# A fifth buffer for gathered rows, a later mask, norm scaling on another engine, and a new order of all instructions

## The chip, the cores and the metric

The kernel runs on one core of a Trainium2 chip. The metric is the device time of one execution in microseconds (us). Of three runs of the kernel before, the median is 3445.88 us (3432.36 to 3452.61).

The engines' names: PE is TensorE (matmuls; PEld are its weight loads), DVE is VectorE, ACT is ScalarE, POOL is GpSimd, SP is SyncE, which issues most transfers. Each engine works through a queue of its own, in order, and waits on semaphores for the others.

## The reference

One layer of a hybrid network over 1024 latent tokens with a prefix of 256 context tokens, width 1024, all in float32:

```python
h  = modulate(x, norm1_g, mod[:, 0], mod[:, 1])         # rms_norm(x, g) * (1 + scale) + shift
hc = modulate(ctx, norm1_g, mod_c[:, 0], mod_c[:, 1])
rq, rk, rv, rg, dq, dk, dv = split(h @ w_in)            # the same of hc for the context
ret  = bidirectional retention of 4 heads, chunks of 128 (scores * decay mask), rms_norm, * silu(rg)
diff = attention of 4 head pairs: (softmax(q1 k1) - lam * softmax(q2 k2)) @ v, rms_norm
x  = x + mod[:, 2] * (concat([ret, diff]) @ w_out)
h2 = modulate(x, norm2_g, mod[:, 3], mod[:, 4])
x  = x + mod[:, 5] * peer_ffn(h2)

def block_fn(hb):                                        # peer_ffn, per block of 128 tokens
    q = (hb @ w_query).reshape(t, 8, 2, 128)
    s = einsum('thpc,hpnc->thpn', q, sub_keys)
    v1, i1 = top_k(s[:, :, 0], 16); v2, i2 = top_k(s[:, :, 1], 16)
    best, pos = top_k(v1[..., :, None] + v2[..., None, :], 16)      # of 256 sums
    experts = (i1 * 128 + i2) at pos; gate = softmax(best)
    act = gelu(einsum('thkd,td->thk', expert_u[experts], hb))
    return einsum('thk,thkd->td', gate * act, expert_v[experts])
```

There are 16384 experts, each a row of 1024 numbers in `peer_u` and one in `peer_v`. Each token uses 8 heads x 16 = 128 of them.

## The kernel before, in words

Tokens go in 8 blocks of 128 (the context in two more). The program is written as Python generators, but not run in that order. A class `Plan` records every operation as a node, and a list scheduler fixes the order of each engine's queue ahead of time from estimated costs; it tries several passes and keeps the best by its own estimate. All instructions are then issued from one line, so that nearly every row of the profile says L590, and tiles, not lines, tell operations apart. What steers the scheduler are tables of numbers: QSPAN, ASPAN, GSPAN, LSPAN, HSPAN (where in a stage the generators of another stage are woven in), HOLD (a stretch of planned time in which POOL issues no gathers), PACES (due times of the gathers' steps), `bufs` (how many buffers each tag has in SBUF).

The stages:

- Start: the conditioning vectors `cc` go through silu into `sc`, and `mm<-wst,sc` matmuls make the modulation from chunks of `w_mod`. `norm_rows` loads a block of tokens, sums its squares on ACT in two halves, adds the halves on DVE, takes the power -1/2 on POOL, and multiplies the block by that scale. It is called 18 times: five times into a tile of tag `k`, five into `gat`, eight into `wst`. Transposes on PE (`mm<-ident,k` and the like) follow.
- Input projections (each float32 product as three products of split numbers), rotary embedding, retention for the 4 retention heads with the decay mask, attention for groups of blocks [0], [4, 5], [6, 7], [3], [1, 2]. `late_queries` computes some of the queries later (`mm<-wst,rv`, 256 columns).
- `route`, `top16`, `select`: for a block, the scores against the sub-keys and the three top-16 searches. `select` is a run of short DVE instructions on tiles `sel`, ending in `egb` (indices and gates). POOL adds the candidate sums for it.
- Blocks 0, 1 and 2 fetch their experts' rows: `halves` and `gather` issue 768 indirect transfers of 128 rows x 1024 numbers on POOL. A row of `peer_u` is used by one DVE instruction (`gat<-gat,h2t`, a product and its sum), a row of `peer_v` by another (`acc<-gat,act,acc`). Nearly all land in a tile of tag `gat`, which has four buffers and is free again after that DVE instruction; 20 land in buffers lent by tag `h`.
- Blocks 3 to 7 use all experts densely: `gates` writes their gates as a table `Wd`, `dense_act` (128 chunks) splits the chunk's weights on ACT (`CAST h<-wst`) and DVE (`TENSOR_TENSOR h<-wst,h`, the low part) and multiplies (`mm<-k,h`, `mm<-v,h`), `dense_val` multiplies by `peer_v`. This dense phase ends the program; the gathers' DVE work runs beside it.

Of the kernel before, what the change touches and what calls it, by code (L numbers as in the profile page):

```python
# [11 lines left out]
AF = mybir.ActivationFunctionType  # L12
OP = mybir.AluOpType
# [17 lines left out]
PASSES, SHARES = 7, (0.3, 0.5)  # L31
HOLD = [1000, 1550]
EXTRA = [[], [], []]
# [18 lines left out]
LATE = [2, 4, 7]  # L52
QSPAN = [[-0.2, 0.475], [0.1, 1], [-0.1, 1.309], [-0.35, 1.05], [0.15, 0.9]]
ASPAN = [[0.05, 1.424], [0.05, 1.05], [0.15, 1], [0, 1.104]]
GSPAN = [[0.3, 1], [-0.15, 0.754], [0.15, 1.248], [-0.1, 1.2], [-0.3, 0.02]]
DSPAN = [0.02, 0.0, 0.05]
LSPAN = [[0.479, 1.05], [0.565, 1.218], [0.436, 1.3], [0.05, 0.85]]
G2SPAN = [0.182, 0.991]
VL, CL, EC, XE = 'D', 'D', 'D', 'PPPPPPPP'
POFF, PACES = 40, [[0, 3.6], [200, 2.25], [300, 1.17], [700, 1.18], [1100, 1.9]]  # L60
DENSE = [3, 4, 5, 6, 7]
# [6 lines left out]
W0 = [0.552, 1.085]  # L68
HSPAN = [[-0.25, 1.0], [0.05, 0.796], [0.2, 1.588]]
XT = ['gat'] * 5  # L70
# [91 lines left out]
class Plan:  # L162
# [169 lines left out]
    def schedule(self):  # L332
# [77 lines left out]
        while left_n:  # L410
# [22 lines left out]
            for e in engs:  # L433
# [159 lines left out]
def row_bcast(ap, n, offset=0):  # L593
    return bass.AP(tensor=ap.tensor, offset=ap.offset + offset, ap=[[0, 128], [1, n]])


def layer(tc, I, out, dbg=None):
# [3 lines left out]
    with sp as S, pp as P, dp as DR:  # L601
        bufs = {"mm": 8, "h": 8, "k": 5, "rv": 4, "b": 4, "v": 5, "sel": 3, "wst": 4, "gat": 4, "fin": 2,  "u1": 3, "u2": 2, "u3": 2,
                "o": 1, "vi": 2, "egb": 3, "pt": 2, "m4": 4, "s1": 2, "act": 2,  "gsum": 2, "rs": 2, "ssum": 2, "ff": 3}

# [6 lines left out]
        nc = Plan(tc, pools, bufs, {"mm": RESERVE})  # L611
# [4 lines left out]
        def sb(shape, tag, dt=F32):  # L616
            return nc.tile(shape, dt, tag)
# [38 lines left out]

        cc = sb([128, KD, 2], "cc")
        nc.sync.dma_start(cc[:, :, 0], I["c"].rearrange("o (p k) -> (o p) k", k=KD))
# [16 lines left out]
        def norm_rows(kb, tag):  # L675
            lat = kb >= NCB
            src = I["x"][0, (kb - NCB) * 128:(kb - NCB + 1) * 128, :] if lat else I["ctx"][0, kb * 128:(kb + 1) * 128, :]
            xt = sb([128, D], tag)
            nc.sync.dma_start(xt, src)
            junk = ps([128, 512])  # L680
            ms = sb([128, 3], "m4")
            for i in range(2):
                nc.scalar.activation(junk, xt[:, i * 512:(i + 1) * 512], AF.Square, scale=1.0 / 32.0,
                                     accum_out=ms[:, i:i + 1])
            nc.vector.tensor_tensor(out=ms[:, 0:1], in0=ms[:, 0:1], in1=ms[:, 1:2], op=OP.add)
            rstd(ms[:, 2:3], ms[:, 0:1])
            nc.vector.tensor_scalar(xt, xt, ms[:, 2:3], None, op0=OP.mult)
            return xt
# [3 lines left out]
        nc.tensor.transpose(rt, rows, ident[0:24, 0:24])  # L692
        rcol = sb([128, 24], "rcol")
        nc.vector.tensor_copy(rcol, rt)
# [57 lines left out]
        nc.sync.dma_start(sinr, I["k_sin"])  # L752
        dist = sb([128, 2, 128], "vi")
        nc.sync.dma_start(dist, I["k_dist"])
        lg = sb([128, 2, H], "lg")
# [4 lines left out]
        nc.sync.dma_start(lamp.rearrange("p a h -> p (a h)"), row_bcast(I["diff_lambda"], 256))  # L760
        retg = sb([128, 512], "pt")
        nc.sync.dma_start(retg, row_bcast(I["ret_norm_g"], 512))
        difg = sb([128, 512], "difg")
# [3 lines left out]

        t8 = sb([128, 6, 8], "t8")
        lx = lg.rearrange("p a h -> p (a h)")
# [22 lines left out]
        nc.scalar.activation(gC, lg, AF.Exp, scale=128.0)  # L792
        mask = sb([128, H, 128], "pt")
        for h in range(H):
            nc.vector.tensor_scalar(mask[:, h, :], dist[:, 0, :], lg[:, 0, h:h + 1], None, op0=OP.mult)
            nc.vector.scalar_tensor_tensor(mask[:, h, :], dist[:, 1, :], lg[:, 1, h:h + 1], mask[:, h, :],
                                           op0=OP.mult, op1=OP.add)
        nc.scalar.activation(mask, mask, AF.Exp)
        nc.vector.tensor_scalar(mask, mask, SC, None, op0=OP.mult)

# [93 lines left out]
        rv = [rvs[i // 2][:, i % 2, :] for i in range(NKB)]  # L894
# [464 lines left out]
        u2 = I["peer_u"][0]  # L1359
# [57 lines left out]
        def gates(b):  # L1417


            pt, key = pairs[b]  # L1420

            for g in range(128 // TG):
                stage = [sb([128, 32, TG], "gat" if g % 2 else "rv") for _ in range(4)]
                for q in range(TG // 4):
# [207 lines left out]
```

## Time and profile before

| | |
|---|---|
| median of three runs | 3445.88 us (3432.36 to 3452.61) |
| profiled execution | 3449.74 us |
| its span on the core | 3447.9 us |
| mean clock granted to TensorE in it | 0.960 |
| PE busy, matmuls | 3151.3 us, 91% of the span, 18240 |
| DVE busy | 2654.8 us, 77% |
| ACT busy | 1330.9 us, 39% |
| POOL busy | 1115.0 us, 32% |
| moved by DMA | 809.69 MB, mean 235 GB/s |

The profile's rows give an operation as `out<-in` by the program's tile names, with its count, its busy time, the mean of one in ns, and the idle time ahead of it with what ended that. A fp32 matmul that the program issues once is often recorded as two. The clock is a share of full speed. The dense phase starts at about 1566 us of the span and takes the rest.

### The profile page before, as it was taken

The numbers are of one execution on the slowest core, as the hardware profiler recorded it, in microseconds if no ns is written. First come the engines' busy times: TensorE is split into PE (matmuls) and PEld (weight loads), VectorE is DVE, ScalarE is ACT, GpSimd is POOL, SyncE is SP. The second block draws the span as 40 slices with busy tenths as digits, with TensorE's granted clock in tenths as the row PEclk, the third lists the DMA queues.
The fourth block names the chain that finished last, engine by engine and source line by source line (L and its number), as shares of the span: only waits on it lengthen the run. The fifth ranks groups of instructions, "written<-read, shape, count | busy, mean of one in ns | idle before, by whom it ended". The sixth has DMA issues, their size and how long they took to land. (4 is left out here: it accounts for less than half of the span.)

```text
span 3447.9 us, 51507 instructions
## 1 busy us (share of the span) xinstructions
PE 3151.3 (91%) x18240; PEld 2732.3 (79%) x18240; DVE 2654.8 (77%) x5963; ACT 1330.9 (39%) x3535; POOL 1115.0 (32%) x1099
## 2 busy tenths in 40 slices
PE   7999997779789888897899999999999999999998
PEld 4998575557677766887788888989898889788887
DVE  4457546879997978666978888788888887878797
ACT  4342443425269898753212222222222222222221
POOL 0101111443440201103544444344444443444341
PEclk9999998889999998999999999999999999999999
DMA  5322655777584642654888889798888887878886
GB/s 184 97 82 88 214 194 169 262 272 238 182 292 155 217 138 93 219 194 159 287 296 275 308 273 307 244 305 282 298 287 310 278 307 271 283 258 296 284 289 207
DMA packets 314532, 809.69 MB, mean 235 GB/s; under 512 B 29313, under 2 KB 125593, under 8 KB 314274
## 3 DMA queue, kind: packets, MB, share of 16 engines
q1 hardware_dynamic: 203682, 403.70, 35.1%
q0 software_dynamic: 110592, 402.70, 34.3%
q8 instruction: 144, 2.36, 0.3%
q14 instruction: 114, 0.93, 0.1%
HBM read 745.46 MB, written 60.83 MB: 234 GB/s over the span
## 5 line engine op out<-in xcount | busy, mean ns | idle before, releaser
L590 PE MATMUL mm<-k,h 128*128 128x384 f32 (+1 forms) x4096 | 925.5, 311 | 34.4 <-DVE h L590 32.1
L590 PEld LDWEIGHTS mm<-k,h 128*128 128x128 f32 x4096 | 700.0, 189 | 46.9 <-DVE h L590 33.8
L590 POOL DMA_INDIRECT gat<-peer_v,egb x379 | 465.2, 1227 | 640.8 <-DVE acc L590 432.2
L590 ACT CAST h<-wst 128x512 fp32r<-128x512 f32 (+1 forms) x384 | 286.6, 762 | 895.4 <-PE mm L590 869.3
L590 PE MATMUL mm<-v,h 128*128 128x384 f32 (+1 forms) x2048 | 632.1, 309 | 0.0
L590 POOL DMA_INDIRECT gat<-peer_u,egb x369 | 439.0, 1190 | 589.4 <-DVE gat L590 386.1
L590 PE MATMUL mm<-h,rv 128*128 128x512 f32 x2304 | 602.1, 399 | 17.5 <-DVE rv L590 12.4
L590 DVE SCALAR_TENSOR_TENSOR acc<-gat,act,acc 128x1024 f32<-128x1024 f32 x376 | 483.2, 1285 | 64.1 <-DMA gat<-peer_v,egb 62.6
L590 PEld LDWEIGHTS mm<-h,rv 128*128 128x128 f32 x2304 | 425.1, 190 | 119.4 <-DVE rv L590 21.4
L590 DVE SCALAR_TENSOR_TENSOR gat<-gat,h2t 128x1024 f32<-128x1024 f32 x369 | 452.3, 1231 | 48.2 <-DMA gat<-peer_u,egb 47.8
L590 DVE TENSOR_TENSOR h<-wst,h 128x512 fp32r<-128x512 f32 (+1 forms) x384 | 329.3, 867 | 204.9 <-issue 109.4
L590 PE MATMUL mm<-h,t 128*128 128x512 f32 (+1 forms) x1600 | 419.8, 393 | 26.8 <-DVE b L590 16.9
L590 PEld LDWEIGHTS mm<-v,h 128*128 128x128 f32 x2048 | 387.5, 189 | 7.9
L590 PEld LDWEIGHTS mm<-h,t 128*128 128x128 f32 x1600 | 294.4, 189 | 100.3 <-DVE b L590 22.7
L590 POOL TENSOR_TENSOR m<-m,mhalf 128x4 f32<-128x4 f32 (+1 forms) x78 | 75.5, 970 | 771.2 <-DVE m L590 761.5
L590 PE MATMUL mm<-b,wst 128*128 128x256 f32 (+1 forms) x1280 | 237.3, 340 | 0.6 <-ACT h L590 0.3
L590 PEld LDWEIGHTS mm<-b,wst 128*128 128x128 f32 x1280 | 204.0, 192 | 24.3 <-ACT u L590 2.6
L590 ACT CAST rv<-aT 128x384 fp32r<-128x384 f32 x128 | 65.8, 514 | 355.8 <-DVE aT L590 349.8
L590 DVE TENSOR_TENSOR b<-b,mm 128x512 f32<-128x512 f32 x248 | 164.9, 682 | 43.8 <-PE mm L590 43.6
L590 PE MATMUL mm<-t,h 128*128 128x256 f32 x992 | 186.8, 287 | 6.7 <-DVE aT L590 3.5
L590 PEld LDWEIGHTS mm<-t,h 128*128 128x128 f32 x992 | 158.1, 193 | 8.0 <-DVE aT L590 3.7
L590 PE MATMUL mm<-wst,h 128*128 128x256 f32 x560 | 156.5, 297 | 0.0
(239 smaller groups left out, 4714.5 us busy)
## 6 DMA issues: line engine op xcount, KB each, us to landing
wst<-peer_u_cols SPq DMA_DIRECT2D x128, 512.0 KB, 7.1
wst<-peer_v_halves SPq DMA_DIRECT2D x128, 512.0 KB, 4.5
wst<-w_query_chunks SPq DMA_DIRECT2D x80, 512.0 KB, 5.3
h<-Wd SPq DMA_DIRECT2D x64, 512.0 KB, 9.7
wst<-w_mod_chunks SPq DMA_DIRECT2D x48, 512.0 KB, 5.2
wst<-w_out_chunks SPq DMA_DIRECT2D x40, 512.0 KB, 7.1
Wd<-rv SPq DMA_DIRECT2D x40, 512.0 KB, 6.8
Wd<-gat SPq DMA_DIRECT2D x40, 512.0 KB, 5.7
```

Of the source, the lines that this page charges most:

```text
L590: getattr(handles[n.eng], meth)(*[res(v) for v in a], **k)
```

## The change

- Tag `gat` gets a fifth buffer. The space comes from tiles that live briefly and now share another tag's buffers: the gates' one-hot tile (`o` to `t7`), `cc` (to `u0`), `rcol` and `t8` (to `s1`), the mask (`pt` to `t4`) and the retention norm's gain (`pt` to `t6`).
- The decay mask (eight DVE instructions, an exponential on ACT, a scaling on DVE) and the loads of its distances and of the retention norm's gain are recorded in `retention()`, no longer at the start.
- `norm_rows` multiplies by its scale on ACT (`activation`, Copy) instead of DVE, 18 instructions.
- The tables HOLD, QSPAN, LSPAN, PACES and HSPAN change in some entries, and with these and all of the above the scheduler's order of every engine.

```diff
-HOLD = [1000, 1550]
+HOLD = [1000, 1500]
...
-POFF, PACES = 40, [[0, 3.6], [200, 2.25], [300, 1.17], [700, 1.18], [1100, 1.9]]
+POFF, PACES = 40, [[0, 3.96], [200, 2.25], [300, 1.17], [700, 1.06], [1100, 1.9]]
...
-        bufs = {"mm": 8, "h": 8, "k": 5, "rv": 4, "b": 4, "v": 5, "sel": 3, "wst": 4, "gat": 4, "fin": 2,  "u1": 3, "u2": 2, "u3": 2,
-                "o": 1, "vi": 2, "egb": 3, "pt": 2, "m4": 4, "s1": 2, "act": 2,  "gsum": 2, "rs": 2, "ssum": 2, "ff": 3}
+        bufs = {"mm": 8, "h": 8, "k": 5, "rv": 4, "b": 4, "v": 5, "sel": 3, "wst": 4, "gat": 5, "fin": 2,  "u1": 3, "u2": 2, "u3": 2,
+                "vi": 2, "egb": 3, "pt": 2, "m4": 4, "s1": 2, "act": 2,  "gsum": 2, "rs": 2, "ssum": 2, "ff": 3}
...
-            nc.vector.tensor_scalar(xt, xt, ms[:, 2:3], None, op0=OP.mult)
+            nc.scalar.activation(xt, xt, AF.Copy, scale=ms[:, 2:3])
...
-        dist = sb([128, 2, 128], "vi")
-        nc.sync.dma_start(dist, I["k_dist"])
...
-        retg = sb([128, 512], "pt")
-        nc.sync.dma_start(retg, row_bcast(I["ret_norm_g"], 512))
...
-        mask = sb([128, H, 128], "pt")
-        for h in range(H):
-            nc.vector.tensor_scalar(mask[:, h, :], dist[:, 0, :], lg[:, 0, h:h + 1], None, op0=OP.mult)
-            nc.vector.scalar_tensor_tensor(mask[:, h, :], dist[:, 1, :], lg[:, 1, h:h + 1], mask[:, h, :],
-                                           op0=OP.mult, op1=OP.add)
-        nc.scalar.activation(mask, mask, AF.Exp)
-        nc.vector.tensor_scalar(mask, mask, SC, None, op0=OP.mult)
...
         def retention():
+            retg = sb([128, 512], "t6")
+            nc.sync.dma_start(retg, row_bcast(I["ret_norm_g"], 512))
+            dist = sb([128, 2, 128], "vi")
+            nc.sync.dma_start(dist, I["k_dist"])
+            mask = sb([128, H, 128], "t4")
...
-                    o1 = sb([128, 4, 128], "t4" if q % 2 else "o")
+                    o1 = sb([128, 4, 128], "t4" if q % 2 else "t7")
```

The order moves on every engine. Three places are shown, each with the queue's consecutive rows. A number behind a tile's name is its number in the recording, which differs between the two kernels. First, PE's queue at the select of block 0, before: `mm<-wst,sc` is modulation, `mm<-k,t` are attention scores, and the row `mm_5830<-ident_117,u1_5689` transposes what DVE writes behind the select.

```order
L590 MATMUL mm_5675<-ident_117,wst_5539 128x128 x4
L590 MATMUL mm_5694<-wst_5591,sc_201 2x256 x4
L590 MATMUL mm_5694<-wst_5594,sc_201 2x256 x4
L590 MATMUL mm_5750<-k_1456,t1_5637 128x512
L590 MATMUL mm_5752<-k_1456,t1_5637 128x512
L590 MATMUL mm_5771<-k_1456,t1_5637 128x512
L590 MATMUL mm_5773<-k_1456,t1_5637 128x512
L590 MATMUL mm_5830<-ident_117,u1_5689 128x128 x2
L590 MATMUL mm_5836<-ident_117,h_5535 128x128 x4
```

And with the change, from the modulation chunk to the first transposes (`ident,h`) of what DVE writes behind the select:

```order
L590 MATMUL mm_5781<-wst_5691,sc_203 2x256 x4
L590 MATMUL mm_5851<-ident_117,wst_5642 128x128 x4
L590 MATMUL mm_5862<-ident_117,wst_5642 128x128 x4
L590 MATMUL mm_5882<-k_1336,t1_5481 128x256
L590 MATMUL mm_5884<-k_1336,t1_5481 128x256
L590 MATMUL mm_5891<-wst_5728,rv_5714 128x256 x4
L590 MATMUL mm_5891<-wst_5853,rv_5714 128x256 x4
L590 MATMUL mm_5922<-wst_5728,rv_5864 128x256 x4
L590 MATMUL mm_5922<-wst_5853,rv_5864 128x256 x4
L590 MATMUL mm_5959<-k_1435,t1_5481 128x512
L590 MATMUL mm_5961<-k_1435,t1_5481 128x512
L590 MATMUL mm_5975<-ident_117,h_5772 128x128 x4
```

Eight transposes of a token block (`ident,wst_5642`) and 16 late-query matmuls (`wst,rv`) now stand between the modulation chunk and the transposes that follow the select.

Second, PE's queue at the select of block 5, before, where `mm_8626<-ident_117,sel_8349` transposes the select's result:

```order
L590 MATMUL mm_8591<-k_1456,t1_8502 128x512
L590 MATMUL mm_8593<-k_1456,t1_8502 128x512
L590 MATMUL mm_8626<-ident_117,sel_8349 128x128 x2
L590 MATMUL mm_8641<-wst_8582,rv_7547 128x256 x4
L590 MATMUL mm_8641<-wst_8589,rv_7547 128x256 x4
L590 MATMUL mm_8626<-ident_117,sel_8349 128x128
L590 MATMUL mm_8684<-k_1456,t1_8502 128x512
L590 MATMUL mm_8686<-k_1456,t1_8502 128x512
L590 MATMUL mm_8692<-ident_117,u2_8653 128x128
```

With the change, up to the first of those transposes (now `mm_8803<-ident_117,sel_8455`):

```order
L590 MATMUL mm_8697<-k_1336,t1_8452 128x256
L590 MATMUL mm_8699<-k_1336,t1_8452 128x256
L590 MATMUL mm_8706<-wst_8565,rv_7454 128x256 x4
L590 MATMUL mm_8706<-wst_8604,rv_7454 128x256 x4
L590 MATMUL mm_8731<-wst_8565,rv_7627 128x256 x4
L590 MATMUL mm_8731<-wst_8604,rv_7627 128x256 x4
L590 MATMUL mm_8757<-ident_117,b_8141 128x128 x4
L590 MATMUL mm_8762<-wst_8565,rv_7789 128x256 x4
L590 MATMUL mm_8762<-wst_8604,rv_7789 128x256 x4
L590 MATMUL mm_8786<-ident_117,b_8141 128x128 x4
L590 MATMUL mm_8796<-ident_117,b_8233 128x128 x4
L590 MATMUL mm_8803<-ident_117,sel_8455 128x128
```

Before, the late-query matmuls (`wst,rv`) follow the transposes of `sel`; now 48 of them stand ahead, 24 in these rows and 24 just before them.

Third, DVE's queue at the start of the dense phase, the end of the select of the last block, before. `h<-wst,h` is the low part of a dense chunk's weights:

```order
L590 SCALAR_TENSOR_TENSOR gat_15850,act_5890<-gat_15850,h2t_5016 128x1024
L590 TENSOR_TENSOR sel_15868<-sel_15586,sel_15264 128x800
L590 SCALAR_TENSOR_TENSOR acc_7331<-gat_15853,act_5890,acc_7331 128x1024
L590 SCALAR_TENSOR_TENSOR gat_15858,act_5890<-gat_15858,h2t_5016 128x1024
L590 TENSOR_REDUCE sel_15264<-sel_15868 128x4x4
L590 TENSOR_TENSOR sel_15879<-sel_15586,sel_15264 128x800
L590 SCALAR_TENSOR_TENSOR acc_7331<-gat_15865,act_5890,acc_7331 128x1024
L590 TENSOR_REDUCE sel_15264<-sel_15879 128x4x4
L590 SCALAR_TENSOR_TENSOR gat_15870,act_5890<-gat_15870,h2t_5016 128x1024
L590 CAST egb_15886<-sel_15264 128x128
L590 TENSOR_TENSOR h_15890<-wst_15427,h_15626 128x1024
L590 SCALAR_TENSOR_TENSOR gat_15874,act_5890<-gat_15874,h2t_5016 128x1024
```

With the change, a stretch in the middle of the same select:

```order
L590 MAX sel_15258<-sel_15339 128x8
L590 MATCH_REPLACE s1_15578<-sel_15258,sel_15339 128x50
L590 TENSOR_TENSOR h_15439<-wst_15079,h_15439 128x512
L590 SCALAR_TENSOR_TENSOR acc_7346<-gat_15482,act_5984,acc_7346 128x1024
L590 MAX sel_15258<-s1_15578 128x8
L590 MAX_INDEX sel_15258<-sel_15258,sel_15339 128x8
L590 TENSOR_TENSOR h_15467<-wst_15297,h_15467 128x512
L590 MAX_INDEX sel_15258<-sel_15258,sel_15339 128x8
L590 TENSOR_TENSOR h_15608<-wst_15331,h_15534 128x1024
L590 MATCH_REPLACE s1_15616<-sel_15258,sel_15339 128x50
L590 MAX sel_15258<-s1_15616 128x8
L590 MAX_INDEX sel_15258<-sel_15258,s1_15578 128x8
```

Before, 67 rows of select and gathers stand between two subtractions `h<-wst,h` of 1024 columns (the last of them `h_15890`); now four of them stand inside the select, after 24 (`h_15608`), 40, 67 and 70 of its rows.

Counts: DVE has 4987 instructions instead of 5005, ACT 3319 instead of 3301; PE, POOL and SP have as many as before. Of the gathers, 745 instead of 748 land in `gat` and 23 instead of 20 in lent buffers. Ahead of the first dense matmul's weights stand 123 gather steps on DVE instead of 115.

More of the change, by code (lines that the diff above doesn't have):

```diff
@@ L52 @@
 LATE = [2, 4, 7]
-QSPAN = [[-0.2, 0.475], [0.1, 1], [-0.1, 1.309], [-0.35, 1.05], [0.15, 0.9]]
+QSPAN = [[0.1, 0.475], [0.1, 1.3], [-0.1, 1.309], [-0.35, 1.05], [0.15, 0.9]]
 ASPAN = [[0.05, 1.424], [0.05, 1.05], [0.15, 1], [0, 1.104]]
@@ L56 @@
 DSPAN = [0.02, 0.0, 0.05]
-LSPAN = [[0.479, 1.05], [0.565, 1.218], [0.436, 1.3], [0.05, 0.85]]
+LSPAN = [[0.479, 1.05], [0.565, 1.218], [0.436, 1.3], [0.2, 0.85]]
 G2SPAN = [0.182, 0.991]
 VL, CL, EC, XE = 'D', 'D', 'D', 'PPPPPPPP'
-POFF, PACES = 40, [[0, 3.6], [200, 2.25], [300, 1.17], [700, 1.18], [1100, 1.9]]
+POFF, PACES = 40, [[0, 3.96], [200, 2.25], [300, 1.17], [700, 1.06], [1100, 1.9]]
 DENSE = [3, 4, 5, 6, 7]
@@ L68 @@
 W0 = [0.552, 1.085]
-HSPAN = [[-0.25, 1.0], [0.05, 0.796], [0.2, 1.588]]
+HSPAN = [[-0.25, 1.0], [0.05, 0.796], [0.2, 1.888]]
 XT = ['gat'] * 5
@@ L654, in rstd @@
             nc.gpsimd.tensor_tensor(out=dst, in0=dst, in1=mhalf[:, :n], op=OP.pow)
-        cc = sb([128, KD, 2], "cc")
+        cc = sb([128, KD, 2], "u0")
         nc.sync.dma_start(cc[:, :, 0], I["c"].rearrange("o (p k) -> (o p) k", k=KD))
@@ L692, in layer @@
         nc.tensor.transpose(rt, rows, ident[0:24, 0:24])
-        rcol = sb([128, 24], "rcol")
+        rcol = sb([128, 24], "s1")
         nc.vector.tensor_copy(rcol, rt)
@@ L765, in layer @@
         nc.vector.tensor_scalar(difg, difg, 1.0 - LAM_INIT, None, op0=OP.mult)
-        t8 = sb([128, 6, 8], "t8")
+        t8 = sb([128, 6, 8], "s1")
         lx = lg.rearrange("p a h -> p (a h)")
@@ L1005, in retention @@
         def retention():
+            retg = sb([128, 512], "t6")
[3 more added lines that the diff above has]
+            mask = sb([128, H, 128], "t4")
+            for h in range(H):
+                nc.vector.tensor_scalar(mask[:, h, :], dist[:, 0, :], lg[:, 0, h:h + 1], None, op0=OP.mult)
+                nc.vector.scalar_tensor_tensor(mask[:, h, :], dist[:, 1, :], lg[:, 1, h:h + 1], mask[:, h, :],
+                                               op0=OP.mult, op1=OP.add)
+            nc.scalar.activation(mask, mask, AF.Exp)
+            nc.vector.tensor_scalar(mask, mask, SC, None, op0=OP.mult)
             kwc = [[sb([128, H, 64], f"u{a + 1}") for i in range(NCB)] for a in range(2)]
```

## The prediction

> **What bounds the kernel now.** I read the totals first, then the clock by slices, then five stretches, and last the waits of the engine that bounds.
>
> ```profile
> span 3447.9 us, 51507 instructions
> PE 3151.3 (91%) x18240; PEld 2732.3 (79%) x18240; DVE 2654.8 (77%) x5963; ACT 1330.9 (39%) x3535; POOL 1115.0 (32%) x1099
> PE   7999997779789888897899999999999999999998
> PEclk9999998889999998999999999999999999999999
> ```
>
> TensorE (PE) is the bound: 91% of the span, so 3447.9 - 3151.3 = 296.6 us of idle time and some time at a lowered clock are all that an order can win. The change adds and removes no matmul. The digits put the idle time in the first half. The stretches (columns: stretch, us, busy PE PEld DVE ACT POOL with counts, PE clock, DMA share, GB/s):
>
> ```profile
> 0.00:600.00 600.00, 537.53 (x3761) 444.52 (x3762) 334.98 (x992) 240.26 (x596) 73.83 (x124) 0.96 0.45 146
> 600.00:1150.00 550.00, 457.18 (x2452) 373.16 (x2450) 476.52 (x1474) 287.07 (x857) 198.22 (x216) 0.92 0.69 235
> 1150.00:1500.00 350.00, 300.88 (x1874) 259.16 (x1875) 266.90 (x848) 304.38 (x1097) 31.38 (x59) 0.90 0.47 158
> 1500.00:1700.00 200.00, 162.64 (x868) 145.88 (x867) 148.58 (x455) 61.86 (x151) 63.12 (x90) 0.90 0.67 219
> 1700.00:3448.00 1748.00, 1693.06 (x9291) 1509.61 (x9289) 1427.87 (x2198) 437.31 (x839) 748.40 (x612) 0.99 0.83 282
> ```
>
> The dense phase (last row) leaves 1748.0 - 1693.1 = 54.9 us idle, the four stretches ahead of it 62.5 + 92.8 + 49.1 + 37.4 = 241.8 us. In the second stretch VectorE (DVE) is busy 476.5 of 550 us, 87%, more than PE's 83%: there DVE is as much the bound as PE. What PE waits for, over the whole span (us in total, times, longest):
>
> ```profile
> PE mm L590 <- DVE u L590: 54.9, 22, 15.9
> PE mm L590 <- DVE h L590: 45.7, 21, 23.9
> PE mm L590 <- DVE sel L590: 16.2, 4, 14.3
> ```
>
> Three single waits of 15.9, 23.9 and 14.3 us hold 54.1 us, and each lies at a select, the run of small DVE instructions that picks the top 16 keys of a block. They are the three places that the new order changes most; the other 241.8 - 54.1 = 187.7 us ahead of the dense phase are many short waits.
>
> **The change, part by part.**
>
> *Place 1, select of block 0.* PE's rows (start, duration, idle before and releaser), and the window around:
>
> ```profile
> 559.33 0.77 PE L590 MATMUL mm<-ident,wst 128*128 128x128 f32 x5 [0.55 <-ACT rv L590]
> 563.57 1.99 PE L590 MATMUL mm<-k,t 64*128 64x512 f32 x8
> 581.47 0.69 PE L590 MATMUL mm<-ident,u 128*128 128x128 f32 x2 [15.91 <-DVE u L590]
> 569.00:595.00 26.00, 10.81 (x41) 8.37 (x42) 18.70 (x37) 3.94 (x9) 4.97 (x5) 0.50 0.37 120
> ```
>
> PE stands 15.91 us until DVE is through the select and writes u, and runs at clock 0.50 after it. The new order puts eight transposes of a token block and 16 more late-query matmuls ahead of that point. A transpose takes 0.77 / 5 = 0.154 us, so 1.2 us. A late-query matmul is recorded twice at 0.232 us (2.32 / 10, the last row quoted for place 2), so 32 x 0.232 = 7.4 us. Two of the four k,t matmuls are half as wide: -0.5 us. The cover grows by 1.2 + 7.4 - 0.5 = 8.1 us. Half of the new matmuls need an eviction that DVE does inside the select; it comes late in it but ahead of the end, so I count them. Idle time left: 15.9 - 8.1 = 7.8 us in two pieces. The 10.81 us of work at half clock would take 5.4 us less at full clock; with 7.8 us of gaps left I count 1. Place 1: -9 us, between 0 and -21.3.
>
> *Place 2, select of block 5.*
>
> ```profile
> 940.77 1.13 PE L590 MATMUL mm<-k,t 64*128 64x512 f32 x4
> 956.24 0.87 PE L590 MATMUL mm<-ident,sel 128*128 128x128 f32 x2 [14.33 <-DVE sel L590]
> 956.89 5.73 PE L590 MATMUL mm<-wst,rv 128*128 128x256 f32 x16
> 963.89 2.32 PE L590 MATMUL mm<-wst,rv 128*128 128x256 f32 x10
> 945.00:960.00 15.00, 3.77 (x10) 2.93 (x11) 14.76 (x29) 3.39 (x7) 13.87 (x8) 0.50 0.84 287
> ```
>
> The transposes of sel stand ahead of late-query matmuls that need nothing of the select (the row at 956.89). In the new order 48 such matmuls stand ahead of them: 96 x 0.232 = 22.3 us of cover for 14.33 us. The most to win is 14.33; I take 10, because DVE is busy 14.76 of 15 us here and the select's end doesn't come earlier, so work behind the select becomes late next. Of the 3.77 us at half clock at most 1.9 come back; I take 1. Place 2: -11 us, between 0 and -16.2.
>
> In the Trainium skill, "TensorE: Matmul & The Clock Gate", Part 1 (The HAM clock gate), the clock falls to half after an idle window of about 3.4 us and comes back after as long a busy one. The trace agrees on the fall: 0.50 in both windows quoted. By that rule a gap left above 3.4 us would keep the half clock, and place 1 would give back the 1 us that I count for it.
>
> *Place 3, start of the dense phase.* PE, its window, and DVE at both ends of the select of the last block:
>
> ```profile
> 1649.07 0.90 PE L590 MATMUL mm<-k,h 128*128 128x384 f32 x2 [23.86 <-DVE h L590]
> 1631.00:1653.00 22.00, 3.93 (x15) 3.93 (x16) 21.90 (x31) 0.00 (x0) 14.95 (x11) 0.50 0.79 243
> 1610.40 0.32 DVE L590 MAX8 sel<-sel 128x8 f32<-128x50 f32 x2
> 1647.79 1.22 DVE L590 TENSOR_TENSOR h<-wst,h 128x1024 fp32r<-128x1024 f32 x1
> ```
>
> DVE runs select and gathers from 1610.40 to 1647.79, 37.4 us, without one subtraction h<-wst,h, and PE's next weights are such an h. The new order sets four of these 1.22 us subtractions into the select, after 24, 40, 67 and 70 of its rows. The 27 rows between the second and the third are the longest way left, 15 us at the pace of before (37.4 us for 67 rows, 0.56 us each), and two chunks lie ready when it begins. Of 23.86 us I count 18 as won; 6 stay, 1.5 us of lateness for each of the four. They push the select itself back by 4.9 us, whose results (gate weights of the last block) aren't needed until later. The 3.93 us at half clock give 2. Place 3: -20 us, between 0 and -25.9.
>
> *The fifth buffer in the dense phase.* Waits from 1700 us on:
>
> ```profile
> PE mm L590 <- DVE b L590: 19.0, 14, 3.6
> PE mm L590 <- DVE rv L590: 11.6, 13, 2.2
> PE mm L590 <- DVE t L590: 8.8, 7, 2.1
> DVE acc L590 <- DMA gat<-peer_v,egb: 59.1, 54, 2.4
> DVE gat L590 <- DMA gat<-peer_u,egb: 25.3, 23, 2.6
> POOL gat L590 <- DVE acc L590: 500.4, 235, 20.0
> POOL gat L590 <- DVE gat L590: 348.1, 170, 7.5
> ```
>
> GpSimd (POOL), which issues the gathers, waits 848.5 us for DVE to free one of the four buffers, so the buffers, not the issuing, set when a gather starts. DVE in turn waits 84.4 us for rows to land, 1.1 us a time and never over 2.6. A fifth buffer lets each gather start about one use earlier: in the dense stretch a step of DVE comes every 1748 / 612 = 2.9 us (POOL's count there, nearly all gathers), more than the longest of these waits. So nearly all 84.4 us go from DVE. DVE is busy 82% here and not the bound; PE gains only what it waits for DVE, 19.0 + 11.6 + 8.8 = 39.4 us, part of which stands behind a DVE that waited for a gather. I take a quarter, 10, as DVE's 84.4 us of such waits are about a quarter of its 1748.0 - 1427.9 = 320.1 us of idle time. Between 0 and -39.4.
>
> *Norm scales, mask, start-up, gathers ahead.*
>
> ```profile
> L590 DVE TENSOR_SCALAR wst<-wst,m 128x1024 f32<-128x1024 f32 x8 | 6.2, 778 | 1.5 <-POOL m L590 1.5
> L590 DVE TENSOR_SCALAR k<-k,m 128x1024 f32<-128x1024 f32 x5 | 3.8, 753 | 3.4 <-POOL m L590 3.4
> L590 DVE TENSOR_SCALAR gat<-gat,m 128x1024 f32<-128x1024 f32 x5 | 3.8, 752 | 1.9 <-POOL m L590 1.9
> L590 ACT ACTIVATE wst<-b 128x1024 f32<-128x1024 f32 x8 | 8.5, 1058 | 55.2 <-POOL b L590 55.2
> 18.72 7.23 PE L590 MATMUL mm<-wst,sc 128*2 128x256 f32 x32 [0.39 <-ACT sc L590]
> 27.34 1.13 DVE L590 SCALAR_TENSOR_TENSOR pt<-vi,lg,pt 128x128 f32<-128x128 f32 x4
> L590 DVE SCALAR_TENSOR_TENSOR acc<-gat,act,acc 128x1024 f32<-128x1024 f32 x376 | 483.2, 1285 | 64.1 <-DMA gat<-peer_v,egb 62.6
> ```
>
> The 18 scales leave DVE (6.2 + 3.8 + 3.8 = 13.8 us) and cost ScalarE (ACT) 18 x 1.058 = 19.0 us, in stretches where ACT is busy 40% and 52%: 0, between -13.8 and +19.0. At the start three scales now stand ahead of sc on ACT, 3.2 us, and PE's first modulation matmuls follow sc; they also wait for their weights, so +1, between 0 and +3.2. The mask's DVE work (1.13 us for one half of it) moves from a place where nothing waits into retention: +1, between 0 and +3. By the new order 123 instead of 115 gather steps stand ahead of the first dense matmul: 8 x 1.285 = 10.3 us more on DVE, most of it where DVE is 87% busy; +3, between 0 and +10.3.
>
> *What a new order gives back.* A new order of everything draws the 187.7 us of short waits anew. The trace can't show the sign; I set one new stall, +15, nearest to the 14.33 us of place 2, between 0 and +32 (two of the mean of the three, 18.0, less some cover).
>
> Sum: -9 - 11 - 20 - 10 + 0 + 1 + 1 + 3 + 15 = -30 us against the profiled execution, whose time is 3449.74 us (span 3447.9 and 1.8 around it): 3419.7, say 3420. That execution is 3.9 us above the median of the three runs, 3445.88, so against the median it is -26 us, 0.8% faster.
>
> **Rivals.**
>
> *B, the fifth buffer does nothing.* For it: the DMA engines are busy 83% in the dense stretch at 282 GB/s, so a fifth gather in flight may only make each land later. Against it: single stretches run higher (0.84 at 287 GB/s in the window of place 2), and DVE's waits are short. Then the -10 goes: 3430.
>
> In the Trainium skill, "DMA: Bandwidth & Descriptors", Specifications gives a core some 358 GB/s of HBM. By that figure the 282 GB/s of the dense stretch leave room, which speaks against B; no run here shows the ceiling.
>
> *C, places 1 and 2 give nothing.* PE does matmuls early there that it did later, but the second stretch ends with DVE, 87% busy, and PE waits for DVE at another point instead. For it: DVE is busy 14.76 of 15 us at place 2. Against it: PE's own 83% is near, and the matmuls moved are needed anyway. The -20 goes: 3440.
>
> *D, slower: a norm scale blocks ACT.* ACT works its queue in order. A scale now waits there for DVE's addition of the two halves and for POOL's power; where that addition stands behind a select, ACT's evictions behind the scale stand too, and PE with them, some 16 us (place 1) each time. Eight of the scales (wst) fall in 290 to 860 us, beside the selects, and at place 1 POOL's power for the second block stands behind POOL's 19 additions for the select. Against it: there the new order has both additions ahead of the long part of the select. Two blocks, 32 us, undo the forecast's gain; three, 48 us, give 3468.
>
> **How the numbers follow.** Chances: forecast 0.45, B 0.15, C 0.25, D 0.15. A measurement of this kernel tells about 0.5% from no change: below 3428.6 counts as faster, above 3463.1 as slower. Faster: 0.42 of the forecast's, half of B (0.08) and a part of C (0.07), 0.57. Same: the rest of these, 0.28. Slower: D, 0.15. The range runs from 3388 (all three places won with their clock, -63.4, would be 3386) to 3460, where the last part of D is left out; the forecast's own range is 3395 to 3428.
>
> **What would show it.** Right: the rows ahead of ident,u (select of block 0), ident,sel (block 5) and the first k,h show waits of at most 8, 4 and 6 us; DVE's waits for gathers in the dense phase fall from 84 to under 25 us and PE's for b, rv and t by about 10; PE busy in the dense phase stays near 1693 us. B would show the gather waits unchanged at a higher DMA share; C a stretch 600 to 1150 as long as before with PE waiting elsewhere; D long ACT waits ended by POOL m. The forecast is wrong if the order search made new stalls of over 15 us, or if gains of the dense phase are much larger than a quarter of PE's waits.

## The result, and the profile after

The changed kernel took 3349.64 us (median of four runs, 3348.43 to 3351.59) against 3439.12 us for the kernel before on the same chip: a ratio of 0.9737, interval 0.9714 to 0.9759. It is 2.6% faster, where the prediction had 0.8% and a range down to 3388 us. The profiled executions tell the same: spans of 3347.3 and 3447.9 us, 100.6 us apart.

The page of the changed kernel, same lines as before:

```profile
span 3347.3 us, 51357 instructions
PE 3126.4 (93%) x18240; PEld 2724.4 (81%) x18240; DVE 2643.7 (79%) x5945; ACT 1346.6 (40%) x3553; POOL 1158.2 (35%) x1099
PE   7999989778989888898999999999999999999998
PEclk9999999879989999999999999999999999999999
```

To find the place I cut both executions at two points that mean the same in any order: the first dense matmul `mm<-k,h`, and the start of the ninth of the 128 dense chunks (257th of 4096 records of `mm<-k,h`). The part from there to the last matmul is called the dense stretch here. In the kernel before the first dense matmul starts at 1537.7 us, not at about 1566 as the text ahead of the prediction has it. Stretches of before, then of the changed kernel (columns as in the prediction):

```profile
1537.70:1686.40 148.70, 115.89 (x617) 103.71 (x616) 118.17 (x325) 40.12 (x74) 59.47 (x86) 0.90 0.63 205
1686.40:3438.60 1752.20, 1706.29 (x9376) 1522.62 (x9374) 1431.55 (x2204) 441.46 (x844) 752.05 (x615) 0.99 0.83 283
```

```profile
1529.40:1651.70 122.30, 111.97 (x604) 99.20 (x603) 118.41 (x327) 37.28 (x75) 65.20 (x86) 0.96 0.73 247
1651.70:3338.10 1686.40, 1685.37 (x9385) 1520.41 (x9383) 1423.72 (x2194) 442.31 (x846) 769.95 (x607) 1.00 0.85 292
```

| stretch | before | changed | difference | the prediction's terms there |
|---|---|---|---|---|
| up to the first dense matmul | 1537.7 | 1529.4 | -8.3 | -9 - 11 + 1 + 1 + 3 + 15 = 0 |
| first eight dense chunks (place 3) | 148.7 | 122.3 | -26.4 | -20 |
| dense stretch | 1752.2 | 1686.4 | -65.8 | -10 |

The dense stretch is where the forecast failed. In the changed kernel PE is busy 1685.37 of 1686.40 us there at full clock: the stretch is at PE's floor. The waits from 1700 us on, in the changed kernel, DVE's for gathers and PE's only row:

```profile
DVE gat L590 <- DMA gat<-peer_u,egb: 7.5, 5, 5.5
DVE acc L590 <- DMA gat<-peer_v,egb: 2.7, 4, 1.2
PE mm L590 <- DVE h L590: 1.0, 1, 1.0
```

DVE's 84.4 us of waiting for rows are 10.2, PE's waits for DVE are 1.0.

### The profile page after: what moved, and what is told of

Its sections match the earlier page's. It is cut to its first block, busy times and chain, and to the rows that moved or that the text cites. A ratio compares the mean times of both kernels' runs of the same rounds, so it can differ in the third digit from the quotient of the medians.

```text
span 3347.3 us, 51357 instructions
## 1 busy us (share of the span) xinstructions
PE 3126.4 (93%) x18240; PEld 2724.4 (81%) x18240; DVE 2643.7 (79%) x5945; ACT 1346.6 (40%) x3553; POOL 1158.2 (35%) x1099
## 4 chain that ended last, share of the span: by engine, by line
PE 56%; DVE 15%; ACT 6%; issue 3%; POOL 2%; DMA 1%; DVEq 0%; POOLq 0%; ACTq 0%
PE mm L590 56%; DVE sel L590 3%; ACT t L590 2%; DVE gat L590 2%; DVE m L590 2%; DVE acc L590 1%; DVE h L590 1%; DVE t L590 1%; ACT rv L590 1%; DVE vi L590 1%; POOL gat L590 1%; ACT gat L590 1%; DMA gat<-peer_u,egb 1%; ACT h L590 1%; DVE s L590 1%
## 5 line engine op out<-in xcount | busy, mean ns | idle before, releaser
L590 PE MATMUL mm<-k,h 128*128 128x384 f32 (+1 forms) x4096 | 911.9, 308 | 0.2 <-DVE h L590 0.2
L590 POOL DMA_INDIRECT gat<-peer_u,egb x365 | 471.2, 1291 | 517.9 <-DVE acc L590 297.8
L590 PE MATMUL mm<-h,rv 128*128 128x512 f32 x2304 | 588.5, 396 | 3.0 <-DVE h L590 1.3
L590 DVE TENSOR_TENSOR b<-b,mm 128x512 f32<-128x512 f32 x248 | 165.5, 682 | 128.8 <-PE mm L590 127.3
L590 PE MATMUL mm<-t,t 128*128 128x128 f32 x1280 | 198.4, 303 | 41.3 <-ACT t L590 29.7
L590 PEld LDWEIGHTS mm<-t,t 128*128 128x128 f32 x1280 | 178.2, 204 | 69.9 <-ACT t L590 50.8
L590 ACT ACTIVATE t<-ob,pt 128x128 f32<-128x128 bf16 x640 | 218.5, 406 | 36.4 <-PE mm L590 17.4
```

The source lines that it names most:

```text
L590: getattr(handles[n.eng], meth)(*[res(v) for v in a], **k)
```

## The experiments

Three theories of the dense stretch: the **buffer** (a fifth row in flight takes DVE's waits away, and each of these waits had gone on to PE), the **order** (the new tables put the gather steps at better places), and that the order before was just an unlucky draw of the search. Numbers are collected in one table behind the texts. "Gather waits" are DVE's for `peer_u` and `peer_v` rows within the dense stretch, "lead" is the number of gather steps (DVE's instructions that use a fetched row) that stand on DVE ahead of the 17th dense chunk's weights, by the order.

### The buffer alone, in one order

`e1_four_buffers` edits one number of the changed kernel; `e3_order_for_four_run_with_five` keeps the order of e1 row for row, and gives the program five buffers (first e1's edit of the changed kernel, then e3's):

```diff
-        bufs = {"mm": 8, "h": 8, "k": 5, "rv": 4, "b": 4, "v": 5, "sel": 3, "wst": 4, "gat": 5, "fin": 2,  "u1": 3, "u2": 2, "u3": 2,
+        bufs = {"mm": 8, "h": 8, "k": 5, "rv": 4, "b": 4, "v": 5, "sel": 3, "wst": 4, "gat": 4, "fin": 2,  "u1": 3, "u2": 2, "u3": 2,
...
-        nc = Plan(tc, pools, bufs, {"mm": RESERVE})
+        nc = Plan(tc, pools, {**bufs, "gat": 4}, {"mm": RESERVE})     # e3: planned for four, run with five
```

> The changed kernel with four gather buffers instead of five, everything else as changed, the order planned anew for four. Theory B (buffer): the dense phase got 66 us shorter (1752 to 1686 us from its 257th k,h matmul to the end) because a fifth row in flight takes DVE's waits for gathers away; then this kernel has the dense stretch back at 1740 to 1755 us, DVE's waits for gathers at 60 us or more, and takes 3405 to 3425. Theory O (order): the new tables place the gather steps better between the dense steps, and the buffer matters little; then the dense stretch is 1685 to 1700 us and the time 3350 to 3375.

> The order of e1_four_buffers word for word (planned for four buffers), but with five buffers in memory. Theory B: the transfers start earlier although no queue has moved, DVE's waits for gathers fall under 20 us, the dense stretch is 1690 to 1700 us and the time 3355 to 3375. Theory O: as e1_four_buffers within 10 us.

e1 took 3429.35 us (ratio to before 0.9966, 0.9947 to 0.9984), e3 3404.25 us (0.9892, 0.9866 to 0.9918). The dense stretch of e1 and DVE's waits for gathers in it, then the same of e3:

```profile
1719.60:3427.60 1708.00, 1695.70 (x9387) 1523.69 (x9387) 1421.52 (x2179) 440.92 (x843) 728.78 (x601) 1.00 0.85 286
DVE acc L590 <- DMA gat<-peer_v,egb: 41.1, 33, 3.3
DVE gat L590 <- DMA gat<-peer_u,egb: 35.3, 30, 4.2
```

```profile
1707.60:3393.40 1685.80, 1685.80 (x9388) 1521.11 (x9386) 1420.82 (x2179) 441.35 (x843) 742.42 (x600) 1.00 0.85 290
DVE gat L590 <- DMA gat<-peer_u,egb: 1.8, 2, 1.1
DVE acc L590 <- DMA gat<-peer_v,egb: 0.2, 1, 0.2
```

With no queue changed, the buffer takes the waits from 76 to 2 us and the dense stretch from 1708.0 to 1685.8. That is theory B's effect, though e3's total is 29 us above the 3375 that B allowed: the rest lies ahead of the stretch. e1 fits neither theory: with four buffers and nearly the waits of before (76 against 84) its stretch is 1708, not B's 1740 and more, and not O's 1700 or less. So the old order lost 44 us that this four-buffer order doesn't.

### The tables

`e4_old_tables` puts all five old tables into the changed kernel, `e7_tables_alone` the five new ones into the kernel before; `e10_paces_alone` and `e10h_hold_alone` put one into the kernel before, `e9_old_paces` and `e8_old_hold` one old one into the changed kernel:

```diff
-HOLD = [1000, 1550]          # e10h: before with the new one; e8: changed with the old one, so the other way round
+HOLD = [1000, 1500]
...
-POFF, PACES = 40, [[0, 3.6], [200, 2.25], [300, 1.17], [700, 1.18], [1100, 1.9]]     # e10; e9 the other way round
+POFF, PACES = 40, [[0, 3.96], [200, 2.25], [300, 1.17], [700, 1.06], [1100, 1.9]]
```

> The changed kernel with all of the old tables (HOLD, QSPAN, LSPAN, PACES, HSPAN), with the fifth buffer, the late mask and the scaling on ACT. Theory B: keeps the 66 us of the dense stretch and loses at most what the order won elsewhere (26 us at the start of the dense phase, 8 ahead of it): 3350 to 3385, dense stretch under 1700. Theory O: loses nearly all, 3415 to 3440, dense stretch above 1735.

> The kernel before with the new tables alone: four buffers, mask early, scaling on DVE. Theory B: dense stretch still 1740 to 1755; only the start of the dense phase may win: 3405 to 3440. Theory O: 3360 to 3385 with the dense stretch under 1700.

> The kernel before with the new PACES alone (the first 200 gather steps due 3.96 instead of 3.6 us of planned time apart, so all later ones 72 us later; the last 68 at 1.06 instead of 1.18). With all new tables the dense stretch was 1698 us at four buffers instead of 1752. Theory PA: it is PACES, which gives dense steps precedence over gather steps on DVE: dense stretch under 1710, time 3395 to 3425. Theory X: it is another table, or just how a search of orders falls: above 1735.

> The changed kernel with the old PACES alone. Theory B (five buffers carry the dense stretch whatever the order): dense stretch 1680 to 1692, DVE's waits for gathers under 20 us, time 3350 to 3390 by what the start of the dense phase does. Theory PA as well as B would give the same in the dense stretch; if the stretch is above 1700, five buffers aren't enough without the new PACES.

> The kernel before with the new HOLD alone (POOL may issue gathers again from 1500 instead of 1550 us of planned time). By the order, 206 instead of 189 gather steps then stand on DVE ahead of the 17th dense chunk's weights, and the lead stays. Theory H (this lead is the slack that let the four-buffer orders with new tables bear 78 us of gather waits at little cost): dense stretch 1695 to 1710 instead of 1752, the first sixteenth of the dense phase 160 to 180 instead of 149 since the lead is paid there, 3400 to 3425 in all. Theory X (another table, or how a search falls): dense stretch above 1735, 3430 and more.

> The changed kernel with the old HOLD alone. Five buffers carry the dense stretch, 1680 to 1692. Theory H2 (HOLD is what shortened the first sixteenth of the dense phase, 122 us, by starting gathers before the last select): first sixteenth 140 to 150, time 3365 to 3385. Theory N (where the last select falls in DVE's order is the search's draw): first sixteenth may be anything from 120 to 175, and the time up to the first dense matmul differs by over 15 us too.

e4 took 3424.74 us (0.9947, 0.9930 to 0.9965), e7 3419.51 (0.9933, 0.9915 to 0.9951), e10 3441.07 (1.0007, 0.9987 to 1.0027), e9 3357.86 (0.9769, 0.9750 to 0.9789), e10h 3431.28 (0.9976, 0.9959 to 0.9992), e8 3410.54 (0.9923, 0.9901 to 0.9945).

All five-buffer orders have the dense stretch at 1680 to 1691 us, old tables or new, as theory B had it for e4, e9 and e8. With four buffers the new tables bring it to 1698.5 (e7: theory O's stretch, but theory B's total), and HOLD alone to 1699.6. PACES alone changed no row of the order, so e10 is a repeat of the kernel before, and theory PA falls. HOLD lets POOL start gathers earlier, so the lead grows from 189 to 206 steps. The lead is paid for at the start of the dense phase. The dense stretch of e10h, and PE's two longest waits near it, both within the first eight chunks (start, duration, idle before and releaser):

```profile
1721.00:3420.60 1699.60, 1688.38 (x9387) 1521.24 (x9386) 1419.21 (x2177) 442.36 (x843) 728.35 (x599) 1.00 0.85 287
1576.38 0.90 PE L590 MATMUL mm<-k,h 128*128 128x384 f32 x2 [26.54 <-DVE h L590]
1624.08 0.90 PE L590 MATMUL mm<-k,h 128*128 128x384 f32 x2 [24.46 <-DVE h L590]
```

That is place 3's kind of stall twice, and the eight chunks take 171.8 us instead of 148.7. So HOLD alone wins 52.6 in the dense stretch, gives 23.1 back at its start and 11.5 ahead of it (47.7, 23.5 and 9.3 against e10, the old order in another execution). Theory H was right on the two stretches (1695 to 1710, 160 to 180); the total is 6 us above its range, by the part ahead of them. But lead and HOLD move together in every four-buffer order here (185 to 189 steps with 1550, 204 to 208 with 1500), and HOLD redraws the whole order; that the lead is what does it is argued, not shown.

e4 and e8 lost 61 us and more although their dense stretch is the best of all. Their first dense matmul starts at 1588.9 and 1575.8 instead of 1529.4, and the eight chunks take 21 us more. That one entry of HOLD redraws the order of the whole program is seen; why the redrawn one is 46 to 60 us longer ahead of the dense phase is not settled. e4's expectation had missed it, and so had theory H2 of e8, which was right on the eight chunks alone (143.7 of 140 to 150); theory N of e8 had allowed for over 15 us there.

### A slower issue of transfers, at fixed orders

If a wait passes on to PE, more waiting must lengthen the stretch. I meant to shorten the transfers: each `peer_v` gather but the first of a block fetches 64 rows instead of 128, which leaves out these experts' part for the other 64 tokens, orders unchanged, on the kernel before (`e11_half_v_gathers`), on e10h (`h11_half_v_hold`) and on the changed kernel (`a11_half_v_changed`).

```diff
...
-                        k["in_offset"] = bass.IndirectOffsetOnAxis(ap=res(k["in_offset"][0]), axis=0)
+                        k["in_offset"] = bass.IndirectOffsetOnAxis(ap=res(k["in_offset"][0])[0:64 if few else 128], axis=0)
+                        k["out"] = k["out"][0:64] if few else k["out"]
...
+                t.base.few = r > 0          # in v_step; DVE's step of such a tile works on 64 rows too
```

> The kernel before, its order of every queue unchanged, but each transfer of peer_v rows (the first of a block apart) fetches only 64 of the 128 rows, and the DVE step that uses it works on these 64; the other tokens' sums lack those experts. DVE's step takes as long as before by its 1024 columns; only the landing is shorter. Theory W (waits pass on): in the old order PE's loss in the dense phase comes from DVE standing for rows that land late; DVE's waits for peer_v fall from 59 us to under 15, the dense stretch from 1752 to 1695 to 1715 and the time to 3380 to 3405. Theory P (position): the dense steps simply stand too late in DVE's order; the dense stretch stays above 1735 and the time above 3420.

> The kernel of e10h_hold_alone (four buffers, gathers 17 steps ahead), order unchanged, with the same halved peer_v transfers. It tells a lead from a buffer. Theory L (the lead of gather steps absorbs waits): waits rise by some 55 us again, from 75 to about 130, but the dense stretch from 1700 only to 1725 or less. Theory 1:1 (each us of waiting costs PE one, whatever the lead): 1745 to 1760.

> The changed kernel, order unchanged, with the edit of e11_half_v_gathers: each peer_v transfer fetches 64 of 128 rows, the other tokens' sums lack those experts. In the old order this raised DVE's waits for gathers in the dense phase from 84 to 140 us, since POOL's issue took 1.5 instead of 1.2 us and the landing was no shorter, and the dense stretch by 57 us. Theory C (five buffers cover a transfer's delay): waits for gathers under 30 us and a dense stretch under 1700, time under 3370. Theory R (POOL's issuing rate is next): waits of 60 us and more, dense stretch 1705 to 1740.

e11 took 3515.98 us (1.0226, 1.0203 to 1.0249), h11 3504.82 (1.0172, 1.0146 to 1.0198), a11 3404.09 (0.9896, 0.9868 to 0.9923). The edit turned against its purpose: the transfers landed no sooner and POOL took longer to issue them (last section). As a dose of waiting it served as well, with the other sign. Stretch and gather waits of e11 (lines are numbered L595 there):

```profile
1698.30:3507.70 1809.40, 1728.07 (x9375) 1537.63 (x9374) 1429.08 (x2203) 441.35 (x844) 903.99 (x615) 0.98 0.77 225
DVE acc L595 <- DMA gat<-peer_v,egb: 82.7, 56, 4.6
DVE gat L595 <- DMA gat<-peer_u,egb: 62.4, 43, 4.1
```

In the old order 60.7 us more waiting made the dense stretch 57.2 us longer (62.1 against e10): nearly one for one. Of the 57.2, 35.4 us are more idle time of PE and 21.8 longer busy time for the same matmuls, at a clock of 0.98 instead of 0.99. So waits do pass on, as W has it, though the kernel moved away from the numbers W named. P isn't refuted whole: its numbers (above 1735 and 3420) hold too, and only its strict form, that the waits don't matter, is out. In h11, with a lead of 206, 86.0 us more waiting cost 64.8 us, three quarters, to 1764: above the limit of 1725 that theory L set, and 4 us above what theory 1:1 had. That order bore its first 75 us of waits at little cost, and the next 86 not. In a11 the waits came back to 81.1 us with five buffers, and the stretch rose by 44.3 to 1730.7, within the numbers of theory R: five buffers cover the normal issue, not the slower one. That POOL's issuing rate is the limit there, as R has it, isn't shown: POOL still stands 597.7 us (312.1 + 285.6) in that stretch until DVE frees a buffer.

### Another draw, the scaling, an earlier HOLD

`n1_other_draw` and `n3_before_other_draw` change only the planner's estimate of a semaphore's delay (`SEM`, 0.18 to 0.19 us) in the changed kernel and in the one before; `e5_scaling_on_dve` undoes the scaling on ACT; `h1450_earlier_gathers` sets HOLD to [1000, 1450].

> The changed kernel with nothing changed but the planner's estimate of a semaphore's delay, 0.19 instead of 0.18 us: another order of the same kernel. If an order is a draw: dense stretch still 1680 to 1692, while the time up to the first dense matmul and the first sixteenth scatter by 10 to 40 us, 3345 to 3395 in all. If the parts decide: 3340 to 3360.

> The kernel before with the planner's semaphore delay at 0.19 instead of 0.18 us, another order of the same kernel; 185 gather steps ahead of the 17th dense chunk, as before (189). Theory L (a small lead and four buffers make the slow dense stretch): 1740 to 1760 us in the dense stretch, 3425 to 3455 in all. Theory N (the old order was an unlucky draw): below 1725.

> The changed kernel with the scaling of norms back on DVE. Theory Z (the move is worth nothing): the time up to the first dense matmul within 15 us of 1529, the dense stretch 1680 to 1692, total 3340 to 3375. Theory S (the move frees DVE where it is the bound): up to 14 us later at the first dense matmul, 3360 to 3380 in all. Theory D (the scale blocks ACT's queue): 10 us or more earlier at the first dense matmul.

> The changed kernel with HOLD ending at 1450: by the order 243 gather steps instead of 197 ahead of the 17th dense chunk. If more lead still wins: dense stretch 1675 to 1683, 3335 to 3345. If the dense stretch is at PE's floor: 1680 to 1688 there, and the steps put ahead cost the start of the dense phase 15 to 45 us: 3360 to 3395.

n1 took 3359.43 us (0.9773, 0.9746 to 0.9800), n3 3418.45 (0.9916, 0.9892 to 0.9941), e5 3369.01 (0.9807, 0.9785 to 0.9829), h1450 3411.94 (0.9928, 0.9903 to 0.9953).

| kernel | buffers | lead | first dense matmul | eight chunks | gather waits | dense stretch |
|---|---|---|---|---|---|---|
| before | 4 | 189 | 1537.7 | 148.7 | 84.4 | 1752.2 |
| e10 (same order) | 4 | 189 | 1539.9 | 148.3 | 84.6 | 1747.3 |
| n3 | 4 | 185 | 1531.8 | 141.0 | 78.6 | 1742.1 |
| e1 | 4 | 204 | 1551.7 | 167.9 | 76.4 | 1708.0 |
| e7 | 4 | 208 | 1535.1 | 174.3 | 78.8 | 1698.5 |
| e10h | 4 | 206 | 1549.2 | 171.8 | 75.0 | 1699.6 |
| e11 (order of before) | 4 | 189 | 1539.9 | 158.4 | 145.1 | 1809.4 |
| h11 (order of e10h) | 4 | 206 | 1549.2 | 184.3 | 161.0 | 1764.4 |
| e3 (order of e1) | 5 | 204 | 1541.2 | 166.4 | 2.0 | 1685.8 |
| e4 | 5 | 182 | 1588.9 | 143.8 | 12.1 | 1680.1 |
| e8 | 5 | 182 | 1575.8 | 143.7 | 12.6 | 1680.1 |
| changed | 5 | 197 | 1529.4 | 122.3 | 10.2 | 1686.4 |
| e9 | 5 | 199 | 1532.4 | 123.8 | 6.4 | 1690.3 |
| n1 | 5 | 201 | 1537.0 | 122.5 | 3.5 | 1688.1 |
| e5 | 5 | 209 | 1532.0 | 135.6 | 3.8 | 1690.8 |
| h1450 | 5 | 243 | 1531.2 | 176.6 | 11.6 | 1691.4 |
| a11 (order of changed) | 5 | 197 | 1529.2 | 126.5 | 81.1 | 1730.7 |

n3 has a small lead, four buffers and a dense stretch of 1742, so another draw has the old order's loss too, which speaks against an unlucky draw; its total fell below the 3425 expected through the parts ahead. n1 shows what another draw does to the changed kernel: 10 us, all stretches within 8 us, so the parts decide; e9 differs by 8 us. The changed order is the fastest that ran. e5 is 19 us slower than the changed kernel, more than these two: the scaling on ACT may be worth something at the start of the dense phase (13 us there), but one draw can't settle it, and theories Z and S both allow its 3369; theory D (it blocks ACT) is out, since the first dense matmul came no earlier. In h1450 a still larger lead wins nothing more in the dense stretch and costs 54 us in the eight chunks, as its second theory had it, though it allowed 45 us there, 1688 for the stretch and 3395 in all.

The eight chunks go with HOLD and the buffers together: about 123 us for five buffers with 1500 (135.6 with the scaling on DVE), 141 to 149 with 1550 for either, 168 to 174 for four with 1500, and 166.4 for the order planned for four even when run with five. There it is the order that was planned with five buffers that counts, not the buffer itself.

## Why the prediction was wrong, point by point

- *The bound, and the places.* Right. PE bounds the kernel, and the stall of place 3 is gone, with no wait over 6.8 us left in the eight chunks; -20 was given, -26.4 measured. The rows of the changed kernel for place 1 (three), place 2 (three) and place 3:

```profile
575.83 1.63 PE L590 MATMUL mm<-ident,wst 128*128 128x128 f32 x8 [4.43 <-ACT wst L590]
585.54 4.98 PE L590 MATMUL mm<-wst,rv 128*128 128x256 f32 x14 [2.32 <-DVE rv L590]
598.64 1.11 PE L590 MATMUL mm<-ident,h 128*128 128x128 f32 x4 [7.07 <-DVE h L590]
929.72 0.55 PE L590 MATMUL mm<-ident,sel 128*128 128x128 f32 x3 [2.49 <-DVE sel L590]
943.03 0.45 PE L590 MATMUL mm<-ident,u 128*128 128x128 f32 x1 [10.01 <-DVE u L590]
968.73 0.27 PE L590 MATMUL mm<-ident,sel 128*128 128x128 f32 x1
1555.72 0.58 PE L590 MATMUL mm<-v,h 128*128 128x256 f32 x1 [6.77 <-DVE v L590]
```

- *Places 1 and 2.* Mis-sized. At place 1 the long wait fell to 7.1 us, but others stand beside it: 4.43 + 2.32 + 7.07 = 13.8 us instead of 15.9. At place 2 the transposes of block 5's select (968.73) wait for nothing now, so the cover worked; but ahead of the late-query matmuls PE waits 2.49 us for block 4's select and 10.01 us for what DVE writes behind it, 12.5 us instead of 14.3. In idle time four us were won there, much as rival C has it, where the -20 had counted 18 of idle time and 2 of clock. The 10.01 us are the kind of stall that the +15 for a new order stood for. All of it together, the part ahead of the dense phase came out 8.3 us below its sum of 0.
- *The fifth buffer in the dense phase* is the term that failed: -10, with an end at -39.4, against -65.8. Of its steps, the first was right: "nearly all 84.4 us go from DVE" (10.2 are left; 2 of 76 where only the buffer differs, e1 to e3). The second, "I take a quarter", was wrong: in the old order added gather waits reached PE almost whole (e11: 57 us for 61). And the end of -39.4 was no bound, because it counted only PE's recorded waits for DVE. PE's idle time in the dense stretch was 1752.2 - 1706.3 = 45.9 us, and its busy time 1706.3 - 1685.4 = 20.9 us longer than the changed kernel's for the same matmuls: work at half clock (27.2 us of it, so 13.6 lost, by the drops listed at the end) and, for the rest, probably waits too short for a row. Together 66.8. The clock stood in the row quoted (0.99 of 1748 us, about 17) and got no term. The prediction had named this as a sign of its being wrong: gains of the dense phase much larger than a quarter of PE's waits. Its range of 3388 at the low end left the buffer's own -39.4 out; with it the end would have been about 3347, but that would have met the measured time by luck, not by the sum.
- *How a wait passes on*, in one instance of before: DVE waits for a row, the product `aT` that stands behind it comes late, ACT's cast of `aT` to `rv` and PE's matmuls with `rv` come late in turn, then the clock halves (two rows of DVE, one of ACT, one of PE, then the stretch behind):

```profile
1787.46 1.23 DVE L590 SCALAR_TENSOR_TENSOR gat<-gat,h2t 128x1024 f32<-128x1024 f32 x1 [1.60 <-DMA gat<-peer_u,egb]
1788.61 0.29 DVE L590 TENSOR_TENSOR aT<-aT,t 128x128 f32<-128x128 f32 x1
1788.99 0.51 ACT L590 CAST rv<-aT 128x384 fp32r<-128x384 f32 x1 [7.51 <-DVE aT L590]
1789.55 2.70 PE L590 MATMUL mm<-h,rv 128*128 128x512 f32 x6 [2.19 <-ACT rv L590]
1790.60:1794.00 3.40, 3.40 (x9) 2.62 (x9) 3.40 (x5) 0.15 (x1) 1.03 (x2) 0.50 1.06 334
```

- *What the share couldn't show.* Whether a wait on DVE costs PE depends on how far DVE is ahead. There is a row for that, DVE waiting for PE in the dense stretch: 43.6 us before, 97.8 in e10h, 127.3 in the changed kernel. With the first, 84 us of gather waits go with some 66 over the floor of about 1686; with the second, 75 us go with 14. That row was in the profile before, and the prediction didn't use it. It is a hint and no measure: a11 has 108.1 us of it, and its 81 us of gather waits still cost 44. The dense stretch of before, of e10h, of the changed kernel and of a11:

```profile
DVE b L590 <- PE mm L590: 43.6, 32, 5.8
```

```profile
DVE b L590 <- PE mm L590: 97.8, 61, 4.4
```

```profile
DVE b L590 <- PE mm L590: 127.3, 51, 5.5
```

```profile
DVE b L595 <- PE mm L595: 108.1, 48, 5.4
```

- *The new order's part there.* The prediction gave it nothing in the dense phase. HOLD alone is worth 52.6 us in the dense stretch with four buffers; every order that ran with the fifth buffer and whole transfers is at 1680 to 1691. The two overlap: either alone removes most of the same 66 us, and e4 and e7 lost much of what they won there elsewhere. No run has the old order itself with five buffers; the nearest are e4 and e8, with the old HOLD and a lead of 182 (1680.1).
- *Rivals.* B (transfers are the limit) is out: the dense stretch moves 292 instead of 283 GB/s and the waits are gone. A `peer_v` row does land later, as B has it (median 6.9 instead of 6.2 us from issue), but the fifth buffer covers more than that. D is out: all of ACT's waits for POOL's norm results come to 2.2 us in the changed kernel. *Scales, mask, start-up, gathers ahead*: small terms, not separated, except that e5 leaves up to 19 us for the scaling. At the start, where +1 was given, PE's first wait grew from 14.26 us, for a load, to 15.24, for ACT's scaled block.

The Trainium skill, "DMA: Bandwidth & Descriptors", Specifications gives some 358 GB/s of HBM for a core, which the prediction set against B; the mean of 292 GB/s that the changed kernel reached stays under it, but single stretches of 20 us went above (390 GB/s from 2196 us in the kernel before, 385 from 2589 us in the changed one), so in these runs the figure is no ceiling.

## What to carry to other kernels

An in-order engine that is busy 82% passes its waits on to the bound engine or absorbs them, and its own waits for that engine hint at which. With few of them (some 43 us here) most of the time that it stood reached the bound; with about 100 us it was between a sixth and somewhat over half. The gap to the floor is the stretch's length less the bound engine's busy time at full clock, so the clock column belongs in the sum, not only PE's recorded waits. Where a buffer and an order can each remove the same wait, undo one at a time, and give the buffer to a fixed order to see what it does by itself.

## What was unexpected of the hardware

- The clock fell after shorter gaps than thought. In the dense stretch of before, seven drops to 0.50 followed gaps between two matmul starts of 2.16, 2.53, 2.56, 2.59, 2.60, 2.71 and 3.98 us; six lasted 3.4 us, the one with the gap of 3.98 lasted 6.8. Other gaps of 2.60 and 2.66 us had none. The drops start at 1790.60, 2029.54, 2138.76, 2947.72, 3012.57, 3077.43 and 3196.89 us, all whole multiples of 3.413 us apart. In the 3.413 us that end at each of these times PE is idle for 1.66 to 2.26 us, and in no other such window at full clock for more than 1.52; the two gaps without a drop lie across two windows. So in this trace it is idle time within a fixed window that counts, about half of it, and not the gap alone. The limit isn't sharp in all runs: in e11 a window with 1.74 us idle ended in a drop, and one with 1.85 didn't. The Trainium skill, "TensorE: Matmul & The Clock Gate", Part 1 names an idle window of about 3.4 us; the runs here show that gaps under it can halve the clock for as long.
- With 64 rows of 4 KB instead of 128 in each `peer_v` transfer, these landed as late as before, and the mean issue took longer. Issue to landing from 1700 us on, before and e11, then the groups of issues over the span, before and e11:

```profile
gat<-peer_v,egb POOLq DMA_INDIRECT x338, 6.2
```

```profile
gat<-peer_v,egb POOLq DMA_INDIRECT x339, 6.2
```

```profile
L590 POOL DMA_INDIRECT gat<-peer_v,egb x379 | 465.2, 1227 | 640.8 <-DVE acc L590 432.2
```

```profile
L595 POOL DMA_INDIRECT gat<-peer_v,egb x379 | 581.8, 1535 | 591.8 <-DVE acc L595 385.7 <-DVE gat L595 117.5 <-issue 32.1
```

The mean issue is 1535 instead of 1227 ns for half the rows. It is a few long ones that raise it: the median is 1097 instead of 1008 ns, the longest 7812 instead of 3154. The `peer_u` transfers, unchanged at 128 rows, took 1332 instead of 1190 ns on average, so the number of rows isn't the whole cause. Why, no run here shows.
